# The S5 preparation of a hybrid decoder trunk in three staggered steps instead of two

## The chip, the cores and the metric

The kernel runs on one core of a Trainium2 chip. The metric is the device time of one execution in microseconds (us). Each core has TensorE (PE, matrix products; PEld is its loading of weights), VectorE (DVE), ScalarE (ACT), GpSimd (POOL) and SyncE (SP), which here issues all transfers (its queue is written SPq). Each engine executes its own instructions in their order, and waits where an instruction needs the result of another engine or of a transfer. PSUM is the memory that PE writes to, in banks; SBUF is the memory of the other operands.

## The reference

The trunk has two layers on 512 tokens of width 1024, in float32. Each layer normalises its input, multiplies it by one wide matrix (`w_in`) and feeds three branches: a Mamba-2 state-space branch (SSD), an S5 branch and a latent attention (MLA, 16 heads, causal). Gates merge them; an output product and a norm follow. The part that matters here is the S5 branch. It has 64 groups of 16 channels, with 64 complex states each:

```python
    step = jnp.exp(log_step.astype(f32))[:, None]
    lr, li = lam_re.astype(f32), lam_im.astype(f32)
    mag = jnp.exp(lr * step)
    ang = li * step
    abar_re, abar_im = mag * jnp.cos(ang), mag * jnp.sin(ang)
...
    bu_re = jnp.einsum('gph,bsgh->bsgp', bb_re, uf)
    bu_im = jnp.einsum('gph,bsgh->bsgp', bb_im, uf)
...
    _, _, xr, xi = lax.associative_scan(complex_combine, (a_re, a_im, bu_re, bu_im), axis=1)
```

The kernel computes this scan in chunks of 8 tokens: what a chunk adds to the state (state products), the scan over the 64 chunks, and what inputs and states give within a chunk.

## The kernel before, in words

Every float32 product is made of three: both operands are split into a high part (by ACT, L66) and the rest (by DVE L78, or by POOL L81), and PE multiplies high by high, low by high and high by low (L116, L117, L119 for the wide products, L61 to L63 for the small ones). A weight tile is loaded into `wf` by SP (L102) and split into `wh` (ACT) and `wl` (DVE or POOL); `wf`, `wh` and `wl` have two buffers each.

In each layer the attention (`mla`) runs first, and the S5 preparation (`s5_prep`) is fed into it: `s5_prep` is a generator, and `mla` calls `fill(n)` at fixed places (L510, L513, and L601 with two or three steps per head) to have its next pieces written into the program. Then `mix` runs the S5 scan, the SSD branch, the gates and the output. The program order is only a starting point: a scheduler of the tile framework places the instructions on their engines by its own estimate of when operands are ready.

`s5_prep` handles the 64 groups in 8 blocks of 8, and each block in 4 steps of 2 groups:

- `block(b)` makes the S5 input product, reverses it in time (`pu`, ACT), stores it (`ud`), reads it back in another layout with eight transfers (`puf`, L325), stores that (L329), loads the coefficients `bc` (L332 to L334) and lets POOL form `pbb` and `pbs`.
- `front(b, s)` has POOL form two tensors of a step by six products and sums: `pw` for the state products and `pv` for the products inside a chunk, and stores `pv` to `odr` (L365).
- `back(b, s)`, one step behind `front`: in step 0 the split of `puf` into `pu2` and a new `pmo`; two transposes of `pw` into `pm` (L377, PSUM); the split of `pm` into `pmh` (ACT) and `pml` (DVE); two pairs of state products into `pM` (L386 with `pmh`, L387 with `pml`). In odd steps also: `pM` is moved to `pmo`; four small products `pk` of `pv` and `pbb` (L395); ACT copies `pk` to `pkf`, DVE adds the diagonal, and four transfers store it to `kpad` (L404). In step 3 `pmo` is stored to `msd` (L406).

`pm` and `pk` share one PSUM bank (tag `pb`), `pM` has another. `pu`, `puf` and `pmo` share two SBUF buffers (tag `pf`); `pu2`, `pmh` and `pml` have one buffer each, `pw`, `pv` and `pkf` two.

In the attention, a head has score products (`aux`, L61 to L63), the masked maximum (`sc`, `mx`, DVE L617), the exponential (ACT), transposes of the scores (L639), their split into `ph` (ACT) and `pl` (DVE), and the products with the values (L649 to L652). The weights of the coming heads are `in_w_uq`, `in_w_ukv` and, for the gates, `in_w_in`. In the page and the rows of the trace the numbers at a name's end are left out, so `pu2` reads `pu`, `pw1` reads `pw` and `pv1` reads `pv`.

Of the kernel before, what the change touches and what calls it, by code (L numbers as in the profile page):

```python
# [9 lines left out]
F32 = mybir.dt.float32  # L10
F32R = mybir.dt.float32r
I32 = mybir.dt.int32
AF = mybir.ActivationFunctionType
ALU = mybir.AluOpType
# [6 lines left out]
P = 128  # L21
# [13 lines left out]
class Trunk:  # L35
# [205 lines left out]
    def s5_prep(self, l, pp):  # L241
        nc, a = self.nc, self.a
# [54 lines left out]
        dT = pt("dT", [P, 16])  # L297
# [10 lines left out]
        yield  # L308
        NB = 2
        et = self.gt  # L310
        pf = lambda nm: pp.tile([P, 512], F32, name=nm, tag="pf", bufs=2)

        bbp = [pt(f"pbb{i}", [P, 8, 32]) for i in range(2)]
        for t in bbp:
# [50 lines left out]
            nc.sync.dma_start(odr[:, gs], v1[:, :, 1:9].rearrange("p g k h -> p g (k h)"))  # L365
            return keep["v"], w1

        def back(b, s, uf, bb, v1, w1):
            if s == 0:
                u = keep["u"] = pp.tile([P, 8, 2, 64], F32R, name="pu2", tag="pu2")  # L370
                self.split(uf.rearrange("p (g c) -> p g c", g=8), u[:, :, 0], u[:, :, 1])
                keep["mo"] = pf("pmo").rearrange("p (g c) -> p g c", g=8)
                nc.gpsimd.memset(keep["mo"][:, :, 0], 0.0)
            u, mo = keep["u"], keep["mo"]
            pm = self.pq.tile([P, 512], F32, name="pm", tag="pb")
            for i in range(NB):
                nc.tensor.transpose(pm[:, i * P:i * P + P], w1[:, i].rearrange("p k h -> p (k h)"), self.ident)  # L377
            mh, ml = (pp.tile([P, NB * P], F32R, name=x, tag=x) for x in ("pmh", "pml"))
            self.split(pm[:, :NB * P], mh, ml)
            if s % 2 == 0:  # L380
                keep["pM"] = self.pq.tile([P, 4, 2, 64], F32, name="pM", tag="pM")
            pM = keep["pM"]
            for i in range(NB):
                g = NB * s + i
                k = slice(i * P, (i + 1) * P)
                nc.tensor.matmul(pM[:, g % 4], mh[:, k], u[:, g], start=True, stop=False)  # L386
                nc.tensor.matmul(pM[:, g % 4, 0], ml[:, k], u[:, g, 0], start=False, stop=True)  # L387
            if s % 2:
                q = 4 * (s // 2)
                self.act_(mo[:, q:q + 4, 1:64], pM[:, :, 0, 0:63])  # L390
                self.tt(mo[:, q:q + 4, 1:64], mo[:, q:q + 4, 1:64], pM[:, :, 1, 0:63], ALU.add)

                pk = self.pq.tile([P, P], F32, name="pk", tag="pb")
                for i in range(4):
                    nc.tensor.matmul(  # L395
                        pk[32 * i:32 * i + 32], bbp[b % 2][:, q + i], v1[:, i, 0:8].rearrange("p k h -> p (k h)"),
                        start=True, stop=True, tile_position=(0, 32 * i),
                    )
                kf = pt("pkf", [P, P], 2)
                self.act_(kf, pk)  # L400
                n = 2 * b + s // 2
                self.stt(kf[:, 0:16], self.diag, dT[:, n:n + 1], kf[:, 0:16], ALU.mult, ALU.add)
                for i in range(4):
                    nc.sync.dma_start(kpad[:, 8 * b + q + i, 112:240], kf[32 * i:32 * i + 16])  # L404
            if s == 3:
                nc.sync.dma_start(msd[b // 4, :, :, 8 * (b % 4):8 * (b % 4) + 8].rearrange("p r g c -> r p g c"), mo)  # L406

        todo = None
        for b in range(8):
            blk = block(b)  # L410
            yield
            for s in range(4):
                vw = front(b, s, *blk)
                if todo:
                    back(*todo)
                todo = (b, s, blk[0], blk[1], *vw)
                yield
        back(*todo)


    def norm_in(self, tt, xt, G):
# [810 lines left out]
```

## Time and profile before

| | |
|---|---|
| median of three runs (lowest to highest) | 1980.36 us (1975.66 to 1982.38) |
| the profiled execution, its own time | 1977.92 us |
| its span | 1976.1 us |
| busy: PE, DVE, ACT, POOL | 1870.3, 1420.3, 914.2, 631.9 us |
| moved by transfers | 219.99 MB |

The profiled execution is 2.4 us below the median. The span is what the profile sees between the first and the last instruction; 1.8 us lie around it. The attention stages, into which the preparation is fed, run from about 60 to 376 us and from 1040 to 1375 us. In a row of the timeline a bracket gives the idle time of the engine just before the instruction and what ended it.

### The profile page before, as it was taken

What the parts mean: (1) busy time and instruction counts of PE and PEld (TensorE: products, weight loads), DVE (VectorE), ACT (ScalarE), POOL (GpSimd) and SP (SyncE); (2) the same over time, 40 slices, a digit from 0 to 9 for tenths busy, and PEclk for the clock granted to TensorE, in tenths of its full rate; (3) what the DMA queues carried; (4) which work ended last, traced back from release to release, by engine and by line L of the source; (5) the groups of instructions that cost most, each with busy time, mean ns of one, the idle gap of its engine ahead of it and who ended that gap; (6) DMA issues with size and microseconds to landing.
All of it is one profiled execution on the core that took longest, in us unless ns stands there. A gap on an engine that the chain in (4) does not pass through costs nothing.

```text
span 1976.1 us, 28153 instructions
## 1 busy us (share of the span) xinstructions
PE 1870.3 (95%) x9880; PEld 1528.1 (77%) x9880; DVE 1420.3 (72%) x2882; ACT 914.2 (46%) x1647; POOL 631.9 (32%) x679
## 2 busy tenths in 40 slices
PE   7898999899999989999998989999999999999998
PEld 5687777687877868888876877776878887788887
DVE  6866566799999857744578566667999996776443
ACT  4355455522555545533332555554235663554331
POOL 1746656201233201201118465661013331012010
PEclk9898998899999999999997999998999999999999
DMA  5343333322321266345233334343332224662541
GB/s 158 94 114 94 108 114 103 119 92 84 128 65 64 75 187 182 92 152 167 90 83 90 111 93 122 100 128 96 96 130 75 74 76 113 183 174 86 171 128 43
DMA packets 136253, 219.99 MB, mean 111 GB/s; under 512 B 39856, under 2 KB 79408, under 8 KB 135600
## 3 DMA queue, kind: packets, MB, share of 16 engines
q1 hardware_dynamic: 136112, 218.19, 37.1%
q8 instruction: 78, 1.28, 0.3%
q14 instruction: 63, 0.52, 0.1%
HBM read 182.08 MB, written 31.33 MB: 108 GB/s over the span
## 4 chain that ended last, share of the span: by engine, by line
PE 60%; DVE 22%; DMA 9%; ACT 3%; issue 2%; POOL 2%; SPq 2%; DVEq 0%; ACTq 0%; POOLq 0%
PE mm L116 15%; PE mm L117 14%; PE mm L119 14%; DMA wf<-in_w_in 3%; DVE wl L78 3%; DVE keep L69 3%; PE mm L61 2%; PE mm L62 2%; PE mm L63 2%; PE aux L61 1%; DVE tmp L69 1%; DVE ms L899 1%; PE aux L62 1%; PE aux L63 1%; DVE sc_t L896 1%
## 5 line engine op out<-in xcount | busy, mean ns | idle before, releaser
L116 PE MATMUL mm<-hh,wh 128*128 128x512 f32 (+1 forms) x1232 | 499.5, 405 | 11.5 <-ACT wh L66 8.0
L66 ACT ACTIVATE wh<-wf 128x1024 fp32r<-128x1024 f32 (+1 forms) x294 | 291.3, 994 | 440.2 <-PE mm L117 227.2
L117 PE MATMUL mm<-hl,wh 128*128 128x512 f32 (+1 forms) x1232 | 492.0, 399 | 0.0
L78 DVE TENSOR_TENSOR wl<-wf,wh 128x1024 fp32r<-128x1024 f32 (+1 forms) x243 | 294.8, 1218 | 188.1 <-ACT wh L66 154.3
L119 PE MATMUL mm<-hh,wl 128*128 128x512 f32 (+1 forms) x1232 | 314.9, 393 | 1.9 <-DVE wl L78 1.9
L116 PEld LDWEIGHTS mm<-hh,wh 128*128 128x128 f32 (+1 forms) x1232 | 236.5, 192 | 72.2 <-ACT wh L66 11.6
L117 PEld LDWEIGHTS mm<-hl,wh 128*128 128x128 f32 (+1 forms) x1232 | 236.2, 192 | 48.5 <-issue 0.5
L119 PEld LDWEIGHTS mm<-hh,wl 128*128 128x128 f32 (+1 forms) x1232 | 228.2, 188 | 52.6 <-DVE wl L78 2.3
L81 POOL TENSOR_TENSOR mg<-mg,tmp 128x512 f32<-128x512 f32 x32 | 77.7, 2431 | 458.1 <-DVE tmp L78 240.5
L81 POOL TENSOR_TENSOR wl<-wf,wh 128x1024 fp32r<-128x1024 f32 (+1 forms) x51 | 108.9, 2135 | 302.6 <-PE mm L119 209.3
L116 PE MATMUL mm<-ah,wh 128*128 128x512 f32 x512 | 200.3, 393 | 0.0
L117 PE MATMUL mm<-al,wh 128*128 128x512 f32 x512 | 199.9, 391 | 0.0
L119 PE MATMUL mm<-ah,wl 128*128 128x512 f32 x512 | 127.6, 390 | 0.0
L116 PEld LDWEIGHTS mm<-ah,wh 128*128 128x128 f32 x512 | 96.2, 188 | 21.4 <-ACT pkf L66 0.7
L117 PEld LDWEIGHTS mm<-al,wh 128*128 128x128 f32 x512 | 96.1, 188 | 20.9 <-issue 1.0
L119 PEld LDWEIGHTS mm<-ah,wl 128*128 128x128 f32 x512 | 95.7, 188 | 19.6
L617 DVE CUSTOM_DVE_ANT_0 sc<-aux,cmask 128x128 f32<-128x128 f32 (+3 forms) x128 | 60.9, 485 | 63.5 <-PE aux L63 62.5
L66 ACT ACTIVATE sc<-sc,nm 128x128 f32<-128x128 f32 (+3 forms) x128 | 70.4, 554 | 13.3 <-DVE nm L73 13.2
L81 POOL TENSOR_TENSOR pv<-pq,ar 128x288 f32<-128x288 f32 x64 | 49.1, 789 | 77.2 <-PE pk L395 68.7
L69 DVE SCALAR_TENSOR_TENSOR keep<-mm,cw,keep 128x511 f32<-128x511 f32 (+2 forms) x96 | 71.1, 740 | 2.0 <-ACT keep L66 1.5
L66 ACT ACTIVATE tmp<-mm 128x512 f32<-128x512 f32 x76 | 44.8, 592 | 56.2 <-PE mm L63 31.5
L81 POOL TENSOR_TENSOR pw<-pbb,ar 128x256 f32<-128x256 f32 x64 | 51.0, 799 | 41.8 <-PE pm L377 41.6
(346 smaller groups left out, 4002.8 us busy)
## 6 DMA issues: line engine op xcount, KB each, us to landing
wf<-in_w_in SPq DMA_DIRECT2D x156, 512.0 KB, 3.6
odr<-pv SPq DMA_DIRECT2D x64, 128.0 KB, 2.0
wf<-in_w_c SPq DMA_DIRECT2D x16, 512.0 KB, 3.4
wf<-in_w_a SPq DMA_DIRECT2D x16, 512.0 KB
wf<-kpad SPq DMA_DIRECT2D x128, 64.0 KB, 6.4
wf<-odr SPq DMA_DIRECT2D x16, 512.0 KB, 7.1
wf<-in_w_glu SPq DMA_DIRECT2D x16, 512.0 KB, 3.4
wf<-in_w_b SPq DMA_DIRECT2D x16, 512.0 KB, 3.8
```

The costliest lines, as they stand in the source:

```text
L61: mm(out, ah, bh, start=start, stop=False)
L62: mm(out, ah, bl, start=False, stop=False)
L63: mm(out, al, bh, start=False, stop=stop)
L66: self.nc.scalar.activation(out, in_, func, **kw)
L69: self.nc.vector.scalar_tensor_tensor(out, in0, s, in1, op0, op1)
L78: self.nc.vector.tensor_tensor(out, a, b, op)
L81: self.nc.gpsimd.tensor_tensor(out, a, b, op)
L116: mm(ps[:m], wh[:, o(i)], bh, start=i == 0, stop=False)
L117: mm(ps[:m], wh[:, o(i)], bl, start=False, stop=False)
L119: mm(ps[:m], wl[:, o(i)], bh, start=False, stop=i == k - 1)
L617: nc.vector.tensor_tensor_reduce(out=sc, in0=ps[:, :n], in1=self.cmask[:, 512 - n:512], op0=ALU.add, op1=ALU.max, scale=1.0, scalar=-3.0e3 ...
L896: nc.vector.tensor_tensor(t1, sc1, s, ALU.mult)
```

## The change

`back` is cut in two. `operands(b, s)` stays one step behind `front`: the split of `puf`, the transposes, the split of `pm`, and in odd steps `pk`, `pkf` and the `kpad` stores. `states(b, s)` comes two steps behind `front`: the state products, `pmo` and the `msd` store. In the program text the order within a step is now `front(s)`, `states(s-2)`, `operands(s-1)`. `pu2`, `pmh` and `pml` get two buffers; `puf` and `pmo` get two each and `pu` one, where the three shared two. The space comes from a ring that is kept for transfers issued by GpSimd, of which the kernel has none. The PSUM banks stay as they are. Every engine has the same instructions, and the same number of them, as before.

```diff
--- before.py
+++ after.py
@@ -308,7 +308,7 @@
         yield
         NB = 2
         et = self.gt
-        pf = lambda nm: pp.tile([P, 512], F32, name=nm, tag="pf", bufs=2)
+        pf = lambda nm: pp.tile([P, 512], F32, name=nm, tag=nm, bufs=2 if nm == "puf" else 1)
 
         bbp = [pt(f"pbb{i}", [P, 8, 32]) for i in range(2)]
         for t in bbp:
@@ -365,18 +365,38 @@
             nc.sync.dma_start(odr[:, gs], v1[:, :, 1:9].rearrange("p g k h -> p g (k h)"))
             return keep["v"], w1
 
-        def back(b, s, uf, bb, v1, w1):
+        def operands(b, s, uf, bb, v1, w1):
+
             if s == 0:
-                u = keep["u"] = pp.tile([P, 8, 2, 64], F32R, name="pu2", tag="pu2")
+                u = keep["u"] = pp.tile([P, 8, 2, 64], F32R, name="pu2", tag="pu2", bufs=2)
                 self.split(uf.rearrange("p (g c) -> p g c", g=8), u[:, :, 0], u[:, :, 1])
-                keep["mo"] = pf("pmo").rearrange("p (g c) -> p g c", g=8)
-                nc.gpsimd.memset(keep["mo"][:, :, 0], 0.0)
-            u, mo = keep["u"], keep["mo"]
             pm = self.pq.tile([P, 512], F32, name="pm", tag="pb")
             for i in range(NB):
                 nc.tensor.transpose(pm[:, i * P:i * P + P], w1[:, i].rearrange("p k h -> p (k h)"), self.ident)
-            mh, ml = (pp.tile([P, NB * P], F32R, name=x, tag=x) for x in ("pmh", "pml"))
+            mh, ml = (pp.tile([P, NB * P], F32R, name=x, tag=x, bufs=2) for x in ("pmh", "pml"))
             self.split(pm[:, :NB * P], mh, ml)
+            if s % 2:
+                q = 4 * (s // 2)
+                pk = self.pq.tile([P, P], F32, name="pk", tag="pb")
+                for i in range(4):
+                    nc.tensor.matmul(
+                        pk[32 * i:32 * i + 32], bbp[b % 2][:, q + i], v1[:, i, 0:8].rearrange("p k h -> p (k h)"),
+                        start=True, stop=True, tile_position=(0, 32 * i),
+                    )
+                kf = pt("pkf", [P, P], 2)
+                self.act_(kf, pk)
+                n = 2 * b + s // 2
+                self.stt(kf[:, 0:16], self.diag, dT[:, n:n + 1], kf[:, 0:16], ALU.mult, ALU.add)
+                for i in range(4):
+                    nc.sync.dma_start(kpad[:, 8 * b + q + i, 112:240], kf[32 * i:32 * i + 16])
+            return b, s, keep["u"], mh, ml
+
+        def states(b, s, u, mh, ml):
+
+            if s == 0:
+                keep["mo"] = pt("pmo", [P, 512], 2).rearrange("p (g c) -> p g c", g=8)
+                nc.gpsimd.memset(keep["mo"][:, :, 0], 0.0)
+            mo = keep["mo"]
             if s % 2 == 0:
                 keep["pM"] = self.pq.tile([P, 4, 2, 64], F32, name="pM", tag="pM")
             pM = keep["pM"]
@@ -389,33 +409,22 @@
                 q = 4 * (s // 2)
                 self.act_(mo[:, q:q + 4, 1:64], pM[:, :, 0, 0:63])
                 self.tt(mo[:, q:q + 4, 1:64], mo[:, q:q + 4, 1:64], pM[:, :, 1, 0:63], ALU.add)
-
-                pk = self.pq.tile([P, P], F32, name="pk", tag="pb")
-                for i in range(4):
-                    nc.tensor.matmul(
-                        pk[32 * i:32 * i + 32], bbp[b % 2][:, q + i], v1[:, i, 0:8].rearrange("p k h -> p (k h)"),
-                        start=True, stop=True, tile_position=(0, 32 * i),
-                    )
-                kf = pt("pkf", [P, P], 2)
-                self.act_(kf, pk)
-                n = 2 * b + s // 2
-                self.stt(kf[:, 0:16], self.diag, dT[:, n:n + 1], kf[:, 0:16], ALU.mult, ALU.add)
-                for i in range(4):
-                    nc.sync.dma_start(kpad[:, 8 * b + q + i, 112:240], kf[32 * i:32 * i + 16])
             if s == 3:
                 nc.sync.dma_start(msd[b // 4, :, :, 8 * (b % 4):8 * (b % 4) + 8].rearrange("p r g c -> r p g c"), mo)
 
-        todo = None
+        todo, done = None, None
         for b in range(8):
             blk = block(b)
             yield
             for s in range(4):
                 vw = front(b, s, *blk)
-                if todo:
-                    back(*todo)
+                if done:
+                    states(*done)
+                done = operands(*todo) if todo else None
                 todo = (b, s, blk[0], blk[1], *vw)
                 yield
-        back(*todo)
+        states(*done)
+        states(*operands(*todo))
 
 
     def norm_in(self, tt, xt, G):
@@ -1219,7 +1228,7 @@
     from concourse.bass_utils import run_bass_kernel_spmd
 
     arrays = layouts(inputs)
-    nc = bacc.Bacc("TRN2", target_bir_lowering=False, num_devices=1)
+    nc = bacc.Bacc("TRN2", target_bir_lowering=False, num_devices=1, dynamic_dma_scratch_size=1024)
     aps = {
         n: nc.dram_tensor(f"in_{n}", v.shape, mybir.dt.from_np(v.dtype), kind="ExternalInput").ap()
         for n, v in arrays.items()
```

The change moves instructions, and the scheduler settles where to. Below are rows of the order, before and after the change: line, operation, output, inputs, size, and in brackets what the instruction waits for. Numbers at a name's end tell buffers and blocks apart.

PE at the start of the second layer, from the transposes that waited at 1062.94 us to the attention's next wide product; first before:

```order
L377 MATMUL pm_11132<-ident_94,pw1_11016 128x128 [waits PE_49,Pool_49]
L377 MATMUL pm_11132<-ident_94,pw1_11016 128x128
L237 MATMUL aux_10666<-tmp_10661,ones_230 128x512 [waits DVE_49]
L386 MATMUL pM_11037<-pu2_11025,pmh_11135 128x128 [waits Activation_49]
L387 MATMUL pM_11037<-pu2_11025,pml_11136 128x64 [waits DVE_49]
L386 MATMUL pM_11037<-pu2_11025,pmh_11135 128x128
L387 MATMUL pM_11037<-pu2_11025,pml_11136 128x64
L395 MATMUL pk_11145<-pv1_11004,pbb0_10589 32x128 [waits PE_49]
L395 MATMUL pk_11145<-pv1_11004,pbb0_10589 32x128 x3
L61 MATMUL mm_10795<-ckh_10668,wh_10786 128x512 [waits Activation_49]
L116 MATMUL mm_10844<-hh_9657,wh_10839 128x512
```

and after the change:

```order
L375 MATMUL pm_11132<-ident_94,pw1_11016 128x128 [waits PE_49,Pool_49]
L375 MATMUL pm_11132<-ident_94,pw1_11016 128x128
L237 MATMUL aux_10666<-tmp_10661,ones_230 128x512 [waits DVE_49]
L406 MATMUL pM_11127<-pu2_11025,pmh_11135 128x128 [waits Activation_49]
L382 MATMUL pk_11139<-pv1_11004,pbb0_10589 32x128 [waits DVE_49]
L382 MATMUL pk_11139<-pv1_11004,pbb0_10589 32x128 x3
L407 MATMUL pM_11127<-pu2_11025,pml_11136 128x64
L406 MATMUL pM_11127<-pu2_11025,pmh_11135 128x128
L407 MATMUL pM_11127<-pu2_11025,pml_11136 128x64
L375 MATMUL pm_11167<-ident_94,pw1_11116 128x128 [waits Activation_49,Pool_49]
L375 MATMUL pm_11167<-ident_94,pw1_11116 128x128
L61 MATMUL mm_10795<-ckh_10668,wh_10786 128x512 [waits Activation_49]
```

The four `pk` products come between the first state product and the others, and the next transposes (`pm_11167`) come before the attention's product L61 instead of 24 rows behind it.

ACT around the weight split that starts at 182.13 us (`wh_2203` before, `wh_2198` after; `ph` and `sc` are the attention's, `v2` and `qh` the next heads'); first before:

```order
L66 ACTIVATE wh_2203<-wf_2202 128x1024 [waits DMAHW3_49,PE_49,Pool_49]
L66 ACTIVATE pmo_2051<-pM_2060 128x4x63 [waits PE_49]
L66 ACTIVATE pkf_2173<-pk_2168 128x128 [waits PE_49]
L66 ACTIVATE ph_1685<-aux_1701 128x256 [waits PE_49]
L66 ACTIVATE pmh_2193<-pm_2190 128x256 [waits PE_49,Activation_49]
L66 ACTIVATE tmp_1537<-aux_1706 64x512 [waits PE_49]
L66 ACTIVATE v2_1902<-mm_1903 128x4x64
L66 ACTIVATE v2_1902<-mm_1920 128x4x64
```

and after the change:

```order
L66 ACTIVATE pmh_2193<-pm_2190 128x256 [waits PE_49]
L66 ACTIVATE pmo_2148<-pM_2150 128x4x63 [waits PE_49]
L66 ACTIVATE qh_1883<-mm_1870 64x512 [waits DMAHW6_49,PE_49]
L66 ACTIVATE ph_1678<-aux_1680 128x512 [waits PE_49]
L66 ACTIVATE sc0_1653,rs_871<-sc0_1653,nm_1648 128x128 [waits DVE_49]
L66 ACTIVATE sc1_1659,rs_871<-sc1_1659,nm_1648 128x256
L66 ACTIVATE sc2_1665,rs_871<-sc2_1665,nm_1648 128x384
L66 ACTIVATE sc3_1671,rs_871<-sc3_1671,nm_1648 128x512
L66 ACTIVATE ph_1678<-aux_1687 128x512 [waits PE_49]
L66 ACTIVATE ph_1678<-aux_1694 128x256 [waits PE_49]
L66 ACTIVATE wh_2198<-wf_2197 128x1024 [waits DMAHW1_49,PE_49,Pool_49]
L66 ACTIVATE pmh_2400<-pm_2397 128x256 [waits PE_49]
```

The `pmh` that stood behind the weight split (`pmh_2193`) stands ten places ahead of it now, with `pkf` three places ahead of that, and the third `ph` is ahead of the split too; the `pmh` behind the split is that of the next step.

SP ahead of the same weight (`wf_2202` before, `wf_2197` after; `qh` and `ql` are the attention's); the end of the train, first before:

```order
L329 DMA u20_581<-puf_1810 128x512 [waits DMAHW5_49,DMAHW6_49,DMAHW4_49,DMAHW3_49]
L404 DMA kpad0_578<-pkf_2030 16x128 x3
L404 DMA kpad0_578<-pkf_2030 16x128 [waits DMAHW7_49]
L406 DMA msd0_580<-pmo_1590 2x64x512 [waits DMAHW0_49]
L365 DMA odr0_579<-pv1_2144 128x2x128 [waits DMAHW1_49,Pool_49]
L365 DMA odr0_579<-pv1_2144 128x2x128 [waits DMAHW2_49,Pool_49]
L102 DMA wf_2202<-in_w_in 128x1024 [waits DMAHW3_49,DVE_49]
```

and after the change:

```order
L325 DMA puf_1805<-ud0_582 16x8x64 [waits DMAHW2_49]
L325 DMA puf_1805<-ud0_582 16x8x64 [waits DMAHW3_49]
L391 DMA kpad0_578<-pkf_2167 16x128 [waits DMAHW4_49,DVE_49]
L391 DMA kpad0_578<-pkf_2167 16x128 [waits DMAHW5_49]
L329 DMA u20_581<-puf_1805 128x512 [waits DMAHW6_49,DMAHW3_49,DMAHW2_49]
L391 DMA kpad0_578<-pkf_2167 16x128 [waits DMAHW7_49]
L391 DMA kpad0_578<-pkf_2167 16x128 [waits DMAHW0_49]
L102 DMA wf_2197<-in_w_in 128x1024 [waits DMAHW1_49]
```

The stores `msd` and `odr` no longer stand directly ahead of the weight; from the weight before (`in_w_ukv`) to this one there are 20 transfers before and 17 after.

## Rows read from the trace of the kernel before

**Rows 1.** page: busy us (share of the span) and instructions of each engine

```profile
PE 1870.3 (95%) x9880; PEld 1528.1 (77%) x9880; DVE 1420.3 (72%) x2882; ACT 914.2 (46%) x1647; POOL 631.9 (32%) x679
```

**Rows 2.** windows: us, busy us (instructions) of PE, PEld, DVE, ACT, POOL, clock, DMA

```profile
325.00:330.00 5.00, 4.55 (x17) 3.76 (x17) 4.90 (x12) 2.73 (x7) 3.20 (x6) 0.50 0.34 93
500.00:660.00 160.00, 156.42 (x845) 127.27 (x844) 151.14 (x243) 89.62 (x150) 51.76 (x35) 0.98 0.23 73
```

**Rows 3.** waits of PE, whole span: us in total, times, longest

```profile
PE pM L386 <- ACT pmh L66: 10.6, 11, 2.6
PE pm L377 <- ACT pkf L66: 9.9, 4, 3.7
PE aux L61 <- DVE mx L617: 7.8, 11, 1.7
PE pM L387 <- DVE pml L78: 5.3, 4, 4.2
PE pm L377 <- POOL pw L81: 2.9, 1, 2.9
PE pM L386 <- DVE pu L78: 2.4, 4, 1.8
```

**Rows 4.** timeline around 183 us: start, duration, engine, line, what [idle before]

```profile
182.13 1.06 ACT L66 ACTIVATE wh<-wf 128x1024 fp32r<-128x1024 f32 x1 [4.68 <-DMA wf<-in_w_in]
...
183.35 0.27 ACT L66 ACTIVATE pkf<-pk 128x128 f32<-128x128 f32 x1
...
183.68 0.69 PE L377 MATMUL pm<-ident,pw 128*128 128x128 f32 x2 [3.68 <-ACT pkf L66]
...
184.46 0.38 ACT L66 ACTIVATE pmh<-pm 128x256 fp32r<-128x256 f32 x1 [0.56 <-PE pm L377]
...
185.02 0.41 DVE L78 TENSOR_TENSOR pl<-aux,ph 128x256 fp32r<-128x256 f32 x1
...
185.49 0.47 PE L650 MATMUL aux<-pl,v 128*64 128x256 f32 x1
```

**Rows 5.** timeline around 325 us, DVE and PE

```profile
325.16 0.08 DVE L617 DVE_READ_ACCUMULATOR2_ANT mx<- 128x1 f32 x1
325.27 0.47 PE L386 MATMUL pM<-pu,pmh 128*128 128x128 f32 x1 [1.57 <-ACT pmh L66]
...
325.54 0.74 PE L61 MATMUL aux<-kh,qh 96*128 96x512 f32 x1
```

**Rows 6.** timeline around 1170 us, PE

```profile
1168.61 0.66 PE L377 MATMUL pm<-ident,pw 128*128 128x128 f32 x2 [2.41 <-ACT pkf L66]
...
1170.48 0.80 PE L61 MATMUL aux<-kh,qh 96*128 96x512 f32 x1 [1.21 <-DVE mx L617]
```

**Rows 7.** timeline around 1124 us, ACT and PE

```profile
1123.43 0.63 ACT L66 ACTIVATE pu<-puf 128x512 fp32r<-128x512 f32 x1 [5.23 <-DMA puf<-ud]
...
1124.84 0.33 PE L386 MATMUL pM<-pu,pmh 128*128 128x128 f32 x1 [1.84 <-DVE pu L78]
```

**Rows 8.** waits of SP's queue, 1105 to 1124 us

```profile
SPq L325 <- DMA msd<-pmo: 4.7, 1, 4.7
```

**Rows 9.** timeline of SP's queue, 161 to 175 us

```profile
161.60 5.12 SPq L325 DMA_DIRECT2D puf<-ud  x8
...
169.92 1.84 SPq L404 DMA_DIRECT2D kpad<-pkf  x4
...
173.51 1.10 SPq L102 DMA_DIRECT2D wf<-in_w_in  x1
```

**Rows 10.** timeline, issue and use of the weight at 243.55 us

```profile
243.55 0.38 SPq L102 DMA_DIRECT2D wf<-in_w_in  x1
...
251.66 1.04 ACT L66 ACTIVATE wh<-wf 128x1024 fp32r<-128x1024 f32 x1
```

**Rows 11.** page's transfers: count, KB each, median us to landing

```profile
wf<-in_w_in SPq DMA_DIRECT2D x156, 512.0 KB, 3.6
```

**Rows 12.** products `pv`, by tile: duration ns min/median/max, first and last start

```profile
L81 POOL TENSOR_TENSOR pv<-pv,pv x64: 787/809/1867, 64.2 to 1344.4; 128x288 f32<-128x288 f32 x64
```

## The prediction

> **What bounds the kernel now.** I read the busy shares first, then two windows, then the waits of TensorE (PE), and last the single instructions around each wait. PE is busy 95% of the span and every other engine 72% or less [rows 1], so the change can win only where PE stands still or runs at the lower clock; it takes no instruction from any engine and no byte from a queue. In the attention stages (about 60 to 376 us and 1040 to 1375 us) PE has its gaps: 325 to 330 us hold 4.55 us of PE work at a granted clock of 0.50 (1.2 GHz), while 500 to 660 us hold 156.42 us in 160 at 0.98 [rows 2]. The waits that name the preparation are state products for `pmh` 10.6, transposes for `pkf` 9.9, state products for `pml` 5.3, transposes for `pw` 2.9 and state products for `pu2` (the page writes `pu`) 2.4 us: 31.1 us, 1.6% of the span [rows 3]. More than that can't be won from waiting; the question is how much of it is real.
>
> **What ends last at these waits.** Most of the time lies in about ten places, and in most of them PE's next instruction waits for something else as well.
>
> - At 183.68 us a transpose has waited 3.68 us for `pkf`. ACT works in order, and its weight split `wh` had itself waited 4.68 us for a transfer, with `pkf` and `pmh` behind it. PE's next attention product (L650, 185.49) needs `pl`, which VectorE (DVE) starts only at 185.02, behind its own half of the late weight's split [rows 4].
> - At 325.27 a state product has waited 1.57 us for `pmh`; the score product behind it, at 325.54, needs the maximum `mx` that ended at 325.24 [rows 5]. Without the state products PE would still stand until about 325.3, so at most some 0.3 of the 1.57 us is their own.
> - At 1168.61 a transpose waits 2.41 us for `pkf`, and the score product behind it waits again, 1.21 us, for `mx` [rows 6]. Two more places read like it.
> - At 1124.84 a state product waits 1.84 us for `pu2`, whose ACT half had waited 5.23 us for the `puf` load [rows 7], and that load had stood 4.7 us in the queue of SyncE (SP) for the transfer `msd<-pmo` [rows 8], since `puf` and `pmo` share two buffers. This one is real.
>
> The cause of the shadowed ones is a weight that comes late: SP issues it behind a train of small transfers of the preparation. Eight `puf` loads take 5.12 us of issue, four `kpad` stores 1.84, and the weight goes out at 173.51 us [rows 9], though ACT is free for it at 177.45 [rows 4].
>
> **The change, part by part.** The sum is made against the profiled execution, 1977.9 us, which is 2.4 us under the median of the runs.
>
> 1. *Work.* The same instructions on every engine: 0. The freed ring had no transfer in it: 0.
> 2. *State products one step later.* By the two orders, the PE work between a step's transposes and its first state product grows from 3.8 to 5.9 us on average (an estimate, from durations of the trace), and places with under 0.8 us fall from 11 to 3. ACT needs 0.38 us for `pmh`, and DVE 0.41 for a split of the same shape (`pl`) [rows 4], so in the steady run the cover is enough either way; the late places count. Of the 10.6 us for `pmh`, about 8 lie where `mx` or `pl` is late next. I take −1.5, with bounds of 0 (all passes on) and −10.6.
> 3. *`pkf` ahead of the late weight, and nearer to the transposes.* Around 183 us `pkf`, `pmh` and the third `ph` stand ahead of the late `wh` on ACT now. PE then has its last value products (L650 and L652, 1.5 us) to do in the hole, and waits for `mx` behind DVE's `wl` after that: −1.5. Two of the other `pkf` waits go, with some 0.5 us that is not shadowed: −0.5. But `pk` still shares one PSUM bank with `pm`, and at six places (one before) under 0.9 us of PE work stands between `pk` and the next transposes, which must wait for its reader `pkf`. The wait of this kind is 2.5 us on average now (9.9 us in 4) [rows 3]; the least is the reader's 0.27 [rows 4]. Most of these places stand where ACT has nothing late, so I take the low end: 6 × 0.27 = +1.6. Together −0.4; bounds −9.9 (all gone) and +13 (6 × 2.5 less 2).
> 4. *`puf` with its own buffers.* Its load no longer waits for `msd<-pmo`, so the wait at 1124.84 goes: −1.8. Bounds −2.4 [rows 3] and 0.
> 5. *SP's queue.* No transfer goes away, but the order shifts. Ahead of the weight at 173.51 stand 17 small ones instead of 20; at 0.46 to 0.64 us each [rows 9] it goes out 1.4 to 1.9 us earlier: −1.5, since the engines stood for it. Ahead of the weight at 243.55 stand 22 instead of 12, 4.6 to 6.4 us more. It is used at 251.66 [rows 10] and takes 3.6 us to land [rows 11], which leaves 4.5 us: 0.1 to 1.9 late, +0.5.
> 6. *GpSimd (POOL).* `pk` comes some 9 us of PE work earlier, which frees `pv` earlier, and POOL runs ahead. It is 32% busy [rows 1], and PE waits for it at one place only (`pw`, 2.9 us), where the order is unchanged: 0. Beside other work one `pv` product took up to 1.87 us against a least of 0.79 [rows 12]; if more of them fall beside the splits `wl` that set the late places, each is later by up to 1.1 us: +0.5.
> 7. *Layer start.* At 1062.94 (`pw`, 2.9 us) and 1079.39 (`pml`, 4.2 us) the same products wait for the same writers as before: 0. There the next transposes stand three products behind `pk` now, ahead of the kv product; the reader's time for that is in item 3.
>
> The Trainium skill ("SBUF — State Buffer", "SBUF: two separate sides") says that GpSimd and a DVE operation with two SBUF inputs lock each other out of a shared pair of ports for a whole instruction. The trace's 1.87 against 0.79 us agrees. It speaks against a change that lets POOL run ahead; by it, each meeting with a `wl` split would cost up to that split's length.
>
> Sum: −1.5 − 0.4 − 1.8 − 1.0 + 0.5 = −4.2, and with the end of the preparation, which comes some 7 us of PE work earlier in each layer and leaves the last head alone, −5. That is 1973 us for a profile like this one, and with the 2.4 us to the median **1975 us**, 0.27% faster. I let the clock stand: it was 0.50 right after PE had stood at 325 us [rows 2], and those holes stay in most places.
>
> A second rule of the Trainium skill bears on it ("Perfetto Trace Analysis", "Optimization Strategy"): the same gap repeating can mean too few buffers in SBUF or PSUM. By that rule the new buffers would take away the waits for `pmh` and leave those for `pkf`, whose resource is the one PSUM bank; that is rival B. The trace agrees where `puf` waited for `msd<-pmo`; at the weights that come late it doesn't.
>
> **The rivals.**
>
> - *B, the stagger works in full.* If the state products hold PE at the ten places, the waits for `pmh`, for `pu2`, the `pml` waits but the one of 4.2, and half of those for `pkf` go: 10.6 + 2.4 + 1.1 + 5 = 19. With fewer holes the clock stays up: 325 to 330 us at 0.50 cost 2.5 us [rows 2], and two to three such windows give 6 more. 1980 − 25 = 1955. For it: 31 us are named. Against: the `mx` rows directly behind.
> - *C, slower: transposes wait for `pkf`.* If the six places where `pk` stands right ahead of the next transposes cost the average 2.5 us each, that is +15, minus the 5 of my sum: 1990. It decides once ACT is late at three or more of them, as it is at 183.68, because everything on ACT stands behind a late `wh`. Against: at the place seen the new order has `pkf` ahead of `wh`.
> - *D, the change doesn't do what it says.* A scheduler makes the order and pulls the state products forward again: 5.9 us behind their transposes, where a step lasts ten (316 us of stage in 32 steps). Then 1980.
>
> **How the numbers follow.** Forecast 0.46 (own range 1969 to 1982), B 0.20, C 0.22, D 0.12. This kernel can tell a change of about 0.3%, 6 us, from none: below 1974.4 is faster, above 1986.3 slower. Faster: B and 0.4 of the forecast, 0.38. Slower: nearly all of C, 0.21. Same: the other 0.41. The range takes in most of B and C: 1956 to 1991.
>
> **What would show it.** If I am right, PE's waits for `pmh` fall to about 5 us, those of score products for `mx` (7.8 us [rows 3]) grow by 3 to 6, no `puf` load waits for `msd`, the wait at 1124.84 is gone, and a low clock after 325 us stays. B would show PE full around 180 and 325 us, and `mx` not grown. C would show over 15 us of transposes waiting for `pkf`. I am wrong at the root if `pmh` falls and `mx` doesn't grow, since then the state products were not shadowed.

## The result and the profile after

The changed kernel takes **1992.5 us** (median of 5 runs, 1989.96 to 1999.48) against 1977.03 us before on the same runs (1975.66 to 1982.38): a ratio of 1.008, with a 95% interval of 1.0059 to 1.0102. It is slower, by 15.5 us or 0.8%. The forecast was 1975, and the range ended at 1991. The profiled execution took 1989.96 us with a span of 1988.2, 12.1 us longer than that of before.

The page of the changed kernel, busy us, share of the span and instructions of each engine, to be set beside [rows 1]:

```profile
PE 1858.9 (93%) x9880; PEld 1519.3 (76%) x9880; DVE 1418.4 (71%) x2882; ACT 912.1 (46%) x1647; POOL 624.0 (31%) x679
```

The work is the same. PE is busy 11.4 us less (its mean clock is a little higher, 0.970 against 0.967), and yet the span is 12.1 us longer: over the whole span PE stood some 23 us more. Where, shows in PE's waits over the whole span (us in total, times, longest), beside [rows 3]:

```profile
PE aux L61 <- DMA qh<-rrh: 11.8, 3, 4.2
PE aux L61 <- DVE mx L626: 11.8, 5, 4.1
PE pm L375 <- ACT pkf L66: 10.2, 3, 4.0
...
PE pk L382 <- DVE pml L78: 6.4, 3, 5.6
PE pM L406 <- ACT v L66: 6.0, 1, 6.0
...
PE pM L406 <- DVE pu L78: 2.6, 3, 1.1
PE pm L375 <- POOL pw L81: 2.5, 1, 2.5
...
PE pM L407 <- DVE pml L78: 2.1, 3, 1.0
...
PE pM L406 <- ACT pmh L66: 0.7, 2, 0.4
```

Three things are to be seen. The waits of state products for `pmh` are all but gone, 0.7 us for 10.6: the stagger does what it says. The sum of the waits that name the preparation is what it was: 31.0 us before and 30.9 after in the two attention stages, since a `pk` product now waits for `pml`, a state product for an ACT queue with `v` in front, and the transposes for `pkf` as much as ever. And the attention waits more for its own: 11.8 us for the copies `qh<-rrh`, which took 3.4 before, and 11.8 instead of 7.8 for `mx`. Taken together PE stands 77.1 us in the two stages (windows 60 to 385 and 1040 to 1385 us) instead of 60.6.

Both late things, the copies and the gate weights behind `mx`, are issued by SP. Waits of SP's queue over the span, first of the kernel before, then of the changed one:

```profile
SPq L365 <- POOL pv L81: 39.9, 21, 8.5
...
SPq L325 <- DMA ud<-pu: 10.6, 10, 1.8
```

```profile
SPq L365 <- POOL pv L81: 63.4, 25, 8.5
...
SPq L325 <- DMA ud<-pu: 25.9, 13, 6.0
```

The queue stands longer with an `odr` store at its head that waits for POOL, and with a `puf` load that waits for the `ud` store, and all that is issued later stands behind. In sum over the two stages it does not stand longer, 400 us before and 399 after: other waits fell, and what matters is which loads stand behind a wait. One such place in the timeline of the changed kernel, SP's queue from 310 us (start, duration, line, what):

```profile
310.06 0.41 SPq L322 DMA_DIRECT2D ud<-pu  x1
310.57 0.40 SPq L102 DMA_DIRECT2D wf<-in_w_ukv  x1
312.24 3.17 SPq L325 DMA_DIRECT2D puf<-ud  x7
315.51 0.55 SPq L559 DMA_DIRECT2D qh<-rrh  x1
...
326.36 1.17 SPq L102 DMA_DIRECT2D wf<-in_w_in  x1
```

and what comes of it on PE, ACT and DVE:

```profile
317.50 0.47 PE L61 MATMUL aux<-kh,qh 96*128 96x128 f32 x1 [4.20 <-DMA qh<-rrh]
```

```profile
333.65 1.06 ACT L66 ACTIVATE wh<-wf 128x1024 fp32r<-128x1024 f32 x1 [3.19 <-DMA wf<-in_w_in]
...
334.74 1.41 DVE L78 TENSOR_TENSOR wl<-wf,wh 128x1024 fp32r<-128x1024 f32 x1 [4.01 <-ACT wh L66]
...
336.41 0.69 PE L61 MATMUL aux<-kh,qh 96*128 96x384 f32 x1 [3.69 <-DVE mx L626]
```

The weight goes out at 326.36 us, where its like went out at 318.60 before. Of these 7.8 us the stage had lost 5.2 by the start of head 12; seven more transfers of the queue stand ahead of the weight. ACT stands 3.19 us for it, DVE 4.01, and PE's score product 3.69 for the maximum that DVE could not make. It is the picture of [rows 5], with longer waits, and PE stands at a score product with no state product before it. At 1320 us, in the second layer, it comes again:

```profile
1317.48 1.06 ACT L66 ACTIVATE wh<-wf 128x1024 fp32r<-128x1024 f32 x1 [3.74 <-DMA wf<-in_w_in]
...
1320.15 0.44 PE L61 MATMUL aux<-kh,qh 96*128 96x384 f32 x1 [4.14 <-DVE mx L626]
```

In the three windows of 5 us from 325 to 340 us the clock is 0.75, 0.94 and 0.50: the low clock after the stall is still there, as forecast.

Read by heads (start of each head's first score product, in us; heads 0 to 15 are the first layer's, 16 to 31 the second's):

| | head 5 | 6 | 10 | 13 | 15 | 16 | 25 | 31 |
|---|---|---|---|---|---|---|---|---|
| before | 177.2 | 199.5 | 269.0 | 321.0 | 357.5 | 1092.1 | 1231.0 | 1337.3 |
| changed | 184.8 | 200.0 | 271.6 | 331.5 | 367.2 | 1097.8 | 1234.9 | 1350.4 |
| changed, one buffer each (e3) | 176.5 | 198.0 | 262.1 | 314.2 | 346.6 | 1091.8 | 1230.1 | 1334.9 |

From head 5 to 6 the changed kernel gains 7 us: that is the place of [rows 4], where `pkf` and `pmh` now stand ahead of the late weight. That only makes good what it had lost at heads 3 to 5: at head 6 it is level with the kernel before. It loses time again at heads 10, 11 and 13 and, in the second layer, at 26 to 29. The last row matters for the experiments: there the first stage ends 10.9 us earlier, and by the next layer only 0.3 are left. A part of that is that SSD products in the mixing stage wait longer for DVE (4.4 us for `keep`, against 0.8 before, in the stretch after the attention); the granted clock from 400 to 500 us is 0.97 there and 1.00 before, and the rest stays open.

### The profile page after: what moved, and what is told of

Read it like the earlier page. It is cut to its first block, busy times and chain, and to the rows that moved or that the text cites. A ratio compares the mean times of both kernels' runs of the same rounds, so it can differ in the third digit from the quotient of the medians.

```text
span 1988.2 us, 28066 instructions
## 1 busy us (share of the span) xinstructions
PE 1858.9 (93%) x9880; PEld 1519.3 (76%) x9880; DVE 1418.4 (71%) x2882; ACT 912.1 (46%) x1647; POOL 624.0 (31%) x679
## 4 chain that ended last, share of the span: by engine, by line
PE 53%; DVE 22%; DMA 13%; ACT 4%; SPq 4%; issue 2%; POOL 2%; DVEq 0%; ACTq 0%; POOLq 0%
PE mm L116 13%; PE mm L117 12%; PE mm L119 12%; DMA wf<-in_w_in 4%; DVE wl L78 4%; PE mm L61 2%; DVE keep L69 2%; PE mm L62 2%; PE mm L63 2%; DVE ms L908 2%; DVE sc_t L905 2%; SPq L325 1%; PE aux L61 1%; DVE ms L907 1%; PE aux L62 1%
## 5 line engine op out<-in xcount | busy, mean ns | idle before, releaser
L61 PE MATMUL aux<-kh,qh 96*128 96x128 f32 (+3 forms) x128 | 45.9, 373 | 23.6 <-DMA qh<-rrh 11.8
L78 DVE TENSOR_TENSOR pl<-aux,ph 128x512 fp32r<-128x512 f32 (+1 forms) x96 | 54.5, 592 | 16.9 <-ACT ph L66 16.7
```

The source lines that it names most:

```text
L61: mm(out, ah, bh, start=start, stop=False)
L78: self.nc.vector.tensor_tensor(out, a, b, op)
```

## The experiments

Each kernel was run beside the kernel before; ratios carry 95% intervals.

**Is it the memset on POOL?** In the trace of the changed kernel the memset of `pmo` had been pulled forward on POOL, where it stood for an earlier `msd` store:

```profile
POOL pmo L398 <- DMA msd<-pmo: 68.3, 10, 9.4
```

The first run takes that wait away and leaves PE's order as it is.

```diff
-                keep["mo"] = pt("pmo", [P, 512], 2).rearrange(...)
-                nc.gpsimd.memset(keep["mo"][:, :, 0], 0.0)
+                keep["mo"] = mos[b % 2]      # two fixed tiles, column 0 zeroed once per layer
```

> The change, with one edit: the zero column of pmo is written once per layer into two fixed buffers instead of by a memset on POOL in each block; the rows of PE, ACT, DVE and SP keep their order, and POOL loses the memsets alone. Theory T (in the changed kernel the memset is pulled forward on POOL, waits there for the store msd<-pmo, 68.3 us in 10 waits, POOL's products and with them the odr stores come late, and SP's queue behind them holds up the qh copies and the gate weights): PE's waits for qh<-rrh fall from 11.8 to about 3.4 us and the time falls by 10 to 15 us, to 1977 to 1982. Rival U (the new order on PE and ACT costs the time, transposes right behind pk waiting for pkf and state products in new places): the POOL waits go, the time stays within 3 us of 1990.

Measured: 1993.26 us, 1.0089 (1.0069 to 1.0109), so nothing. Theory T falls for this kernel. POOL then waits for the `bc` loads instead (9.3 us in the changed kernel):

```profile
POOL pu L81 <- DMA bc<-in_s_bc: 57.4, 13, 8.7
```

**Is it the stagger or the buffers?** The kernel before with the buffers of the change and nothing else:

```diff
-        pf = lambda nm: pp.tile([P, 512], F32, name=nm, tag="pf", bufs=2)
+        pf = lambda nm: pp.tile([P, 512], F32, name=nm, tag=nm, bufs=2 if nm == "puf" else 1)
-   name="pu2", tag="pu2")            /  pf("pmo")                  /  (name=x, tag=x)
+   name="pu2", tag="pu2", bufs=2)    /  pt("pmo", [P, 512], 2)     /  (name=x, tag=x, bufs=2)
```

> The kernel before, with two steps as it was, and only the buffers of the change (pu, puf, pmo apart, pu2, pmh and pml twice, the ring freed). Its memsets stand as early on POOL as in the changed kernel. Theory T: the loss comes with the buffers, so it is slower than before by 8 to 16 us, 1985 to 1993. Rival U: the loss comes with the stagger, so this is within 5 us of before, 1972 to 1982.

> As the kernel with the buffers alone, but the zero column of pmo is written once per layer into two fixed buffers; PE's order is the same as there. Theory T: 10 to 15 us faster than the one with the memsets, 1972 to 1980. Rival U: the same as with the memsets, within 3 us. Rival V (the buffers let SP's queue run in an unlucky order, whatever POOL does): also the same as with the memsets, at about 1988.

Measured: 1995.26 us with the buffers alone, 1.0099 (1.0076 to 1.0122), and 1984.73, 1.0043 (1.0024 to 1.0062), with the zero column written once. So no stagger is needed for the loss. These two kernels have the same order on every engine but for the memsets, so in this order the memset did cost some 10 us, though it cost nothing in the changed kernel. The mirror image, the stagger with one buffer each of `pu2`, `pmh` and `pml`:

```diff
-    name="pu2", tag="pu2", bufs=2)     /  (name=x, tag=x, bufs=2) for x in ("pmh", "pml")
+    name="pu2", tag="pu2")             /  (name=x, tag=x) for x in ("pmh", "pml")
```

> The change with three steps, but pu2, pmh and pml with one buffer again (pu, puf and pmo as in the change). Theory T: the memsets stand where they did, so the time stays within 5 us of the change, 1986 to 1996. Rival U: the state products can't fall a full step behind, the order of PE goes back towards that of before, and 5 us or more of the loss go, 1978 to 1986.

Measured: 1977.24 us, 1.0002 (0.9988 to 1.0016). All of the loss is gone, and with it the waits for the copies:

```profile
PE aux L61 <- DMA qh<-rrh: 1.1, 1, 1.1
```

**Which of the buffers?** One buffer of `pu2` alone (e4), one each of `pmh` and `pml` alone (e5), the split into `pu2` fed from a fixed tile (e6), and e3 with the zero column written once (e7).

> The change with pu2 in one buffer; pmh and pml keep two, and the memsets of pmo stay. Theory P (with a second pu2 the scheduler pulls the split of the next block's puf forward on ACT, where it stands for loads that land later, 31 us in layer 0 and 19 in layer 1 against 11.5 and 10.1 before, with pkf, pmh, ph, qh and the weight splits queued behind it): ACT's waits for puf loads fall under 25 us and the time falls to 1974 to 1983. Rival Q (the second pmh and pml let transposes run ahead, and that costs the time): 1987 to 1996.

> The change with pmh and pml in one buffer each; pu2 keeps two. Theory P: ACT's waits for puf loads stay at 40 us or more and the time stays within 5 us of the change, 1986 to 1996. Rival Q: 1974 to 1983.

```diff
-    self.split(uf.rearrange("p (g c) -> p g c", g=8), u[:, :, 0], u[:, :, 1])
+    self.split(still.rearrange("p (g c) -> p g c", g=8), u[:, :, 0], u[:, :, 1])
```

> The change, but the split into pu2 reads a fixed tile of zeros instead of the loaded puf (the loads still run and are still stored), so ACT has no load to wait for there; the state products are then of zeros. Theory P: without these waits 10 to 16 us go, 1974 to 1983, as with one pu2. Rival R (the loss is the new place of the transfers in SP's queue, qh and weights behind the trains, whoever waits on ACT): within 5 us of the change, 1986 to 1996.

> The change with one buffer each of pu2, pmh and pml (which took 1977), and the zero column of pmo written once per layer into two fixed buffers; PE's order stays. The memsets on POOL wait 49.6 us for msd there. Theory T on POOL (the wait holds products, odr stores and SP's queue): 4 to 10 us faster, 1967 to 1973. Rival (POOL would wait for pk or for bc instead, as it did in the change with the same edit): within 3 us of 1977.

Measured: e4 1985.4 us, 1.0046 (1.0023 to 1.0069); e5 1993.67, 1.0086 (1.0061 to 1.0111); e6 1982.62, 1.0022 (1.0003 to 1.004); e7 1977.88, 1.0006 (0.9985 to 1.0027). At first sight that is theory P, by halves. But its own number fails: ACT's waits at the split of `puf`, named to its loads or to the `kpad` stores, were 44 us in e4 (29.3 and 15.1), the faster one, and 25 us in e5 (10.8 and 14.6), the slower, where P wanted it the other way round. So P is not shown.

**How far does the order alone move the time?** The edits of e2 to e6 (e2b keeps the order of e2) have one thing in common: they make the scheduler settle a new order on every engine. Three runs put the attention's copies on ACT's queue, and one feeds the preparation three and two steps per head instead of two and three.

```diff
-    nc.sync.dma_start(bits(q[2 * p + j][x][64:96]), bits(rr[G][x][o]))
+    nc.scalar.dma_start(bits(q[2 * p + j][x][64:96]), bits(rr[G][x][o]))
```

> The change, with the copies qh<-rrh and ql<-rrl of the attention issued from ACT's queue instead of SP's. Theory R (so far the time goes with PE's waits for qh<-rrh: 1 to 3.5 us in kernels at 1977 to 1983, 6 to 8 in those at 1985, 10 to 14 in those at 1993 to 1995; the copies stand in SP's queue behind puf loads that wait for the ud store, and behind odr and kpad stores that wait for POOL and DVE): the waits for qh<-rrh go to under 3 us and the time falls to 1975 to 1984. Rival S (the copies are only one sign of a schedule that fits the real times badly, and the other late work, weights and pu2 splits, stays): the waits for qh go, the waits for mx or pkf grow in their place, and the time stays at 1987 to 1996.

> The kernel before with the same edit, the copies qh and ql on ACT's queue. Theory R: before waits 3.4 us for them only, so it gains 0 to 4 us, 1973 to 1980, much less than the change does by the same edit. Rival S: the edit lets the scheduler land anywhere, 1970 to 1995.

> The change with one buffer each of pu2, pmh and pml (1977), and the copies qh and ql on ACT's queue. Theory R: there is 1.1 us of such waiting to win, so 1974 to 1980. Rival S: 1970 to 1995.

```diff
-                fill(3 if h % 2 else 2)
+                fill(2 if h % 2 else 3)
```

> The kernel before, fed three steps of the preparation at even heads and two at odd ones instead of two and three. It has no more or fewer buffers and the same steps; it only lets the scheduler settle another order, to see how far times scatter by that. Theory P and R (a cause that the buffers bring): within 6 us of before, 1971 to 1983. Rival S (the order alone moves the time by as much as the change did): 10 us or more from before, to either side.

Measured: the same edit makes the changed kernel faster than it was (1980.94 us, 1.0036 of before, 1.002 to 1.0052), and the kernel before slower (1996.29, 1.01, 1.0081 to 1.012), and e3 slower (1987.41, 1.0067, 1.0052 to 1.0082). The neutral one, e10, gives 1980.94, 1.0031 (1.0018 to 1.0045). By their expectations e8 speaks for theory R and e10 for a cause that the buffers bring; e9 and e11 lie far outside R and within S. As e8, e9 and e11 also make ACT issue the copies, their times need not be the order's alone. Taken with the runs on the buffers, rival S stands: with nearly the same work, a kernel lands anywhere between 1977 and 1996 us when its order is settled anew. An experiment that lets the scheduler choose again can't tell a cause of 15 us.

**With the order fixed.** For the remaining runs each engine's instructions were chained in a given order (issue order only, no added wait for an end), so that the scheduler had no choice. The first has the program and the buffers of the change, and the order of e3 on every engine.

```diff
     with tile.TileContext(nc, schedule_with_timeline_sim=True) as tc:
         trunk(tc, aps, out)
+        pin(tc)      # chains every engine's instructions in the order of e3
```

> The buffers of the change (pu2, pmh, pml twice), with every engine's order fixed to that of the kernel with one buffer each, which took 1977; nothing is computed otherwise. Theory O (the buffers cost nothing by themselves; the time of the change comes from the order that the scheduler settles with them): 1970 to 1980, fifteen below the change. Rival B (the buffers themselves cost, by where the tiles lie or by work that runs ahead on its own): 1986 or more.

Measured: 1976.56 us, 1.0004 (0.9992 to 1.0017). This settles the first question: the buffers cost nothing and bring nothing by themselves; the 15 us are the order that the scheduler chose once it had them.

Then the order of the change, with only SP's queue touched: the copies ahead of the loads.

```diff
  SP, one of six places
+ L559 qh_1463<-rrh_1618, L559 qh_1467<-rrh_1618, L559 ql_1464<-rrl_1619, L559 ql_1468<-rrl_1619
  L325 puf_1805<-ud0_582  (x6)
- L559 qh_1463<-rrh_1618, L559 qh_1467<-rrh_1618, L559 ql_1464<-rrl_1619, L559 ql_1468<-rrl_1619
  L325 puf_1805<-ud0_582  (x2)
```

> The change, with the order of PE, ACT, DVE and POOL fixed as it is, and in SP's queue 24 of the copies qh and ql, in six places, moved from behind the puf loads to just ahead of them; no transfer is added or removed. Theory R (the copies behind the puf loads, which wait for the ud store, are what the new order costs): the waits for qh<-rrh fall from 11.8 to under 4 us and the time by 6 to 12, to 1980 to 1986. Rival S (something else in the order is late next, mx behind a late weight or pkf): the qh waits fall, the mx and pkf waits grow, the time stays within 4 us of 1992.

> The change with one buffer each of pu2, pmh and pml, its order fixed, with 16 of the copies qh and ql moved ahead of the puf loads in SP's queue. It waits 1.1 us for qh, so Theory R gives a gain of 0 to 2 us at most, 1974 to 1979; if the copies held more than PE (ACT and DVE behind them), up to 4.

Measured: 2005.12 us, 1.0141 (1.0117 to 1.0165), the slowest of all; the control g2 1984.07, 1.0043 (1.0026 to 1.0061). The waits for the copies are gone (0.7 us), but moved ahead they stand at the head of the queue themselves, for an ACT that is behind a weight split; waits of SP's queue, of the changed kernel and then of f8:

```profile
SPq L559 <- ACT wh L66: 1.8, 3, 0.6
```

```profile
SPq L559 <- ACT wh L66: 18.9, 4, 5.5
```

and the loads and weights behind them are later still: PE's waits for `mx` go from 11.8 to 16.3 us, those for `pu2` from 2.6 to 10.8. So theory R is not shown: moving the copies by themselves mends nothing, and what their late place costs stays open, since the move adds a wait of its own.

Last, the gate weights. In the kernel before, with its order fixed, four of them go ahead of four to eight small transfers (g1); in the order of the change eleven go ahead of four to ten transfers (g5); in that of e3, four ahead of seven to ten (g6).

```diff
  SP, kernel before, one of three places
  L550 qh, ql, qh, ql
+ L102 wf_2202<-in_w_in
  L329 u2<-puf, L404 kpad<-pkf (x4), L406 msd<-pmo, L365 odr<-pv (x2)
- L102 wf_2202<-in_w_in
```

> The kernel before, with its order fixed on every engine but for four gate weights in SP's queue, which go ahead of the four to eight small stores of the preparation that stood directly ahead of them (at 173.51 us among them). The prediction's reading (late weights behind such trains set the stalls, and the waits named to the preparation are shadowed by them): the weight at 173.51 lands 3 to 4 us earlier, the wait of 3.7 us for pkf at 183.68 falls by as much, and the time by 2 to 5, to 1971 to 1975. Rival (the scatter of the stage absorbs it, or another late transfer takes its place): within 2 us of before.

> The change, with its own order fixed on every engine, except that eleven gate weights in SP's queue go ahead of the four to ten transfers of the preparation (kpad, u, msd, odr, at five places with one later pair of the copies qh and ql) that stood between them and the puf loads. Theory W (in the changed order the gate weights stand behind longer trains, the one at 326.36 us 7.8 us later than before, and ACT, DVE and then PE wait behind them): the waits of score products for mx (11.8 us) fall under 6 and the time falls by 7 to 14, to 1978 to 1986. Rival S (whatever is moved ahead pushes something else, as the copies did): within 4 us of 1992 or slower.

> The change with one buffer each of pu2, pmh and pml, its order fixed, with four gate weights ahead of the seven to ten transfers that stood directly ahead of them. Theory W: there ACT waits 7 us a layer for such weights, 2 to 6 us go, 1971 to 1975. Rival S: 1977 or slower.

Measured: g1 1972.68 us, 0.9976 (0.9962 to 0.9991); g5 1978.2, 1.0007 (0.999 to 1.0024), by the ratios 14 us below the change; g6 **1964.49**, 0.9945 (0.9923 to 0.9966), 11 us below e3 and faster than both kernels. The timeline of g1 at the place of [rows 4] and [rows 9]:

```profile
169.39 0.53 SPq L102 DMA_DIRECT2D wf<-in_w_in  x1
...
177.79 1.04 ACT L66 ACTIVATE wh<-wf 128x1024 fp32r<-128x1024 f32 x1
...
180.00 0.38 PE L377 MATMUL pm<-ident,pw 128*128 128x128 f32 x2
```

The weight goes out 4.1 us earlier and lands 4.3 us after its issue instead of 8.5; ACT splits it without a wait, and the transposes that waited 3.68 us for `pkf` wait for nothing. From head 5 to head 6 this kernel takes 17.5 us instead of 22.2. ACT's waits for gate weights in the second stage (1040 to 1385 us), of the kernel before, of the change, of e3 and of g6:

```profile
ACT wh L66 <- DMA wf<-in_w_in: 6.0, 2, 4.1
```

```profile
ACT wh L66 <- DMA wf<-in_w_in: 14.7, 4, 5.9
```

```profile
ACT wh L66 <- DMA wf<-in_w_in: 7.4, 3, 3.5
```

```profile
ACT wh L66 <- DMA wf<-in_w_in: 4.3, 2, 2.8
```

In g5 no such wait is left in either stage, and PE's waits for `mx` in score products fall from 11.8 to 4.6 us. (The profiled execution of g5 took 1970.08 us, the fastest of its runs; the verdict goes by the median.)

The traces show more about these weights than their place in the queue. In the kernel before and in the changed one, a gate weight that SP issues 0.7 to 4.2 us behind an `msd` store lands 6.4 to 9.1 us after its issue; the others whose landing the profile has take 3.4 to 4.1. ACT's waits for such weights behind `msd` come to 10.1 us in three places before, 21.1 in five places in the changed kernel, 7.9 in two places in e3, and there are none in g5 and g6, whose moved weights pass an `msd` store at five of eleven places and at all four. This is read from the traces and not shown by a run of its own, since no edit moved a weight past the `msd` store alone. Nor does it give the time of every kernel: e2 has 10.0 us of it and takes 1995.

What stays open: moving gate weights is worth 14 us in the order of the change, but 11 in the order of e3 by the same kind of edit, so it is not they alone that set the two orders 15 us apart. By the ratios g5 and g6 still differ by 12 us. In their profiled executions, whose spans differ by 4.5 us, PE stands 68.9 and 52.8 us in the two stages; of those 16 us, 5 are waits for the copies, 7 the attention's other waits and 4 the preparation's. Between the changed kernel and e3 it is 21 us, 11, 3 and 7. That the copies cause their part was tried in f8 and not shown.

## Why the prediction was wrong

- *Where the time lies.* Right in that the waits named to the preparation were mostly not to be won: `pmh` fell by 9.9 us and brought nothing. The sign for it, `mx` growing by 3 to 6 us, came in at 4.0, but by luck. Two of its waits, 3.69 us at 336.41 and 4.14 at 1320.15, are 7.8 of the 11.8 us, and both stand behind a weight that came late in the new order. With these weights put ahead, in g5, `pmh` is as low as in the changed kernel and `mx` is under the 7.8 of before, which was named as the sign against the forecast:

```profile
PE pM L406 <- ACT pmh L66: 0.6, 2, 0.4
...
PE aux L61 <- DVE mx L626: 4.6, 5, 1.5
```

- *The late weight.* g1 shows that it is the root at 183 us, and gains 3.4 us in the median where 2 to 5 were expected. But the train's issue time was only half of it. With the 3.6 us of [rows 11] the weight issued at 173.51 would have landed at 177.1, before ACT was free for it; it took 8.5 us.
- *Items 2 to 4.* The wait at 1124.84 went, and no `puf` load waits for `msd` any more. At 183 us the place gained 7 us instead of 3, after heads 3 to 5 had lost 7.6. `pkf` stayed at 10.2 us. Their sizes were small against what was missed.
- *Item 5, SP's queue, is the step that failed.* It counted the transfers between two weights and the `in_w_ukv` load ahead of each, priced them at 0.46 to 0.64 us each with 3.6 us to land, and came to −1.0. But those loads had moved back themselves. The queue issues 1039 transfers in both kernels; counted from the first, 33 of the 76 loads of `in_w_uq`, `in_w_ukv` and `in_w_in` in the two stages stand 6 to 11 places later in the changed kernel, and only 5 stand 6 or more later in e3. The weight of 173.51 stands 6 places later, not 3 earlier, and goes out 4.0 us later, at 177.50, where the stage is 3.9 us late (head 4) and ACT does not wait for it. The weight of 243.55, priced at +0.5, goes out at 249.62, now behind an `msd` store, and ACT waits 4.40 us for it:

```profile
245.47 0.57 SPq L413 DMA_DIRECT2D msd<-pmo  x1
...
249.62 0.47 SPq L102 DMA_DIRECT2D wf<-in_w_in  x1
...
256.11 1.06 ACT L66 ACTIVATE wh<-wf 128x1024 fp32r<-128x1024 f32 x1 [4.40 <-DMA wf<-in_w_in]
```

Head 9 starts at 251.9 us in both kernels, head 10 2.6 us later in the changed one. In the sum −1.0 stood where late gate weights are worth 14 us in this order (g5), and PE's waits for `qh`, 8.4 us more, were in no term at all, though [rows 10] came from the same queue. The count of late places does not give the time by itself: e2 and e2b have 20 each and lie 10 us apart, and e4 has 32 at 1985.4 us.
- *Item 6.* Waiting for POOL was put at 0, as PE does so at one place only. SP waits for it too, through `odr`, 23.5 us more than before, and what is issued later stands behind. That this wait costs the time is not shown: in g5, 14 us faster, it is longer still, with the weights ahead of it.

```profile
SPq L365 <- POOL pv L81: 71.6, 25, 8.5
```

- *Rival C* had the time, 1990, with the wrong mechanism: transposes wait 10.2 us for `pkf`, not over 15. *Rival D* was nearer in kind, in that the scheduler decides; but its price was put at 0, on the belief that an order settled anew costs what the old one did. The runs show a spread of some 20 us for that, upward from the kernel before.
- *The range* reached to 1991 because the order was given no spread of its own. Of the twelve kernels e1 to e11, e3 and e7 lie within 2 us of before and the other ten 6 to 21 us above; a range for a change that makes a scheduler choose again should take that in.
- *The rule on buffers* in the Trainium skill ("Perfetto Trace Analysis", "Optimization Strategy") says that repeated gaps can mean too few buffers. Here f1 puts a number on it: with the order held, three more buffers are worth 1976.56 against 1977.24 us, no difference that these runs can tell.

## What to carry to other kernels

When one in-order queue issues both the prefetches of the critical work and the small stores of a side job, read that queue first: in which place each prefetch stands, counted from the queue's start, what waits at the head before it, and how long it takes to land there: a gate weight issued close behind a slow store took 6.4 to 9.1 us here, where the median is 3.6. A longer cover between two steps, or more buffers, is worth little where the wait ends with a late prefetch; putting four prefetches ahead of small stores was worth 11 us where the whole rebuilding brought nothing. And where a scheduler settles the order, compare edits with the order held fixed, since letting it choose again moved this kernel by up to 1%.

## What was not expected of the hardware

The `msd` store, 256 KB, takes long to land. In the changed kernel a memset on POOL that needs nothing but the end of that store shows it: the store is issued at 322.83 us and the memset runs at 331.38, 8.6 us later, after waiting 9.26 us. In all ten such waits it is 8.1 to 8.6 us. The `ud` store of the same size took 2.3 us in the median of the kernel before, and 2.7 and 7.0 in the two places of the changed one where the profile has it.

```profile
331.38 0.11 POOL L398 MEMSET pmo<- 128x8 f32 x1 [9.26 <-DMA msd<-pmo]
```

So a second buffer of a stored tile is not free as soon as its store has been issued, and an instruction that is cheap in itself, 0.11 us, can hold an engine's queue for that long. The gate weights that SP issued close behind such a store were late with it, as told above.
